# A blocked transpose on one core: three load slots and two store regions, where there were two and three

## The chip, the cores and the metric

The kernel runs on one core of a Trainium2 chip. The core has five engines that run their own instruction streams: PE (TensorE, here used only to transpose), ACT (ScalarE) and DVE (VectorE), which here only copy, POOL (GpSimd), which here only makes an identity matrix, and SP (SyncE), which here issues every data transfer. Sixteen DMA engines move the data between DRAM and the core's on-chip memory of 128 partitions. PE writes into a second on-chip memory, PSUM. Semaphores order the engines among each other. The metric is the device time of one execution in microseconds; lower is better.

## The reference

```python
def setup_inputs():
    return {"x": np.random.randn(8192, 8192).astype(np.float32)}

def reference(x):
    return np.transpose(x)
```

Every one of the 268.44 MB of x is read once and written once, to the transposed place.

## The kernel before

**Tiles.** x is cut into 128 tiles (T) of 128 rows by 4096 columns: 64 chunks of rows (CH) for the first half of the columns, then 64 for the second. A load (L190) brings one tile of 2 MB, 16 KB per partition. The 4096 columns of a tile are 16 ranges (NR) of 256 columns. PE transposes each range in two steps of 128 by 128 (L346), even columns and odd columns, so that a partition holds two neighbouring rows of the result. Ranges 0 to 7 go to the PSUM tensor `ps0`, which ACT empties, ranges 8 to 15 to `ps1`, which DVE empties (`copies`, L252). A range of one tile, transposed, is a *piece*: 1 KB per partition (`PIECE` = 256 floats).

**Regions.** One piece would be written as runs of 512 bytes. So 16 pieces of one range, from 16 tiles that follow each other, are collected in a *region* and stored together (`store`, L288), in runs of 8 KB. Region w belongs to range w % 16 and takes the pieces of tiles w-15 to w: with each tile exactly one region is closed. The piece of tile w is its *closing piece*; it is copied from PSUM straight into the region (`direct`, L224). The other fifteen waited in the tensor `slots`; DVE brings them into the region with one or two copies (`gather`, L227). After the last tile fifteen regions are left with fewer than 16 pieces each; these are the last stores (`flush`, L97). Where a region reaches over the change from the first half of the columns to the second, it is stored in two transfers.

**Memory.** The tensor `arena` has 86 pieces (86 KB) per partition. In it lie load slots of 16 pieces each and the space for regions. At the start there are four load slots, at 0, 16, 54 and 70; the last two are given up early (`over`, L79), and from tile 11 on loads alternate between two slots, at 0 and 16. The pieces from 32 on, 54 of them (`FIN`), are for regions: three full regions follow each other at 32, 48 and 64. A plan made while the program is built (L102 to L147) fixes where each load and each region lies (`home`) and which earlier users of that place must be done (`before`): for a load, that PE has finished the tile that lay there; for a region, that the store of what lay there has landed.

**Order.** SP issues loads and stores from one list (`order`, L102) on one queue: the store of region t-1, the load of tile t+2 (t+4 and t+3 at the start, `lead`, L70), the store of region t, and so on. SP waits at each for its semaphores, so what stands behind waits too. On DVE, `work` (L372) gives for each tile: the gather of its region (which waits until the place is free, then until both engines' copies of the tile before are done), and then the copies of `ps1`. ACT copies `ps0`; it waits for the gather first, since the region's place must be free before the closing piece goes there. Both take their copies in the order of the ranges, as PE finishes 4 ranges (`steps`, L173). The store of a region waits for all copies of the half that has its closing piece (`s_cp`, L292).

**PE's program.** The transposes of tiles 0 to 11 (E = 12) are written out. Tiles 12 to 125 run in a loop whose body is two tiles (L361 to L365), because the load slots alternate by two; it has 57 turns. Tiles 126 and 127 are written out again. For each tile PE waits for the load (L343) and, twice, for an emptied half of PSUM (L341).

Of the kernel before, what the change touches and what calls it, by code (L numbers as in the profile page):

```python
# [40 lines left out]
def kernel(  # L41
# [5 lines left out]
    nc = tc.nc  # L47
    P = 128
# [4 lines left out]
    B = 2  # L53
    NR = 16
# [2 lines left out]
    CH = N // P  # L57
    T = (M // J) * CH
    PIECE = B * P
    FIN = 54  # L60
    QR = NR // 4
    E = 12
    assert CH % W == 0

    FOUR, THREE = 5, 10
    END = 2 * NR + FIN

    def lead(t):  # L70
        return 4 if t < FOUR else 3 if t < THREE else 2


    line = {}
    for t in range(T):
        for u in range(t + lead(t) + 1):
            line.setdefault(u, u if t == 0 and u < 4 else line.get(u - lead(t)))
    ends = sorted((max(t for t in range(T) if t in line and line[t] == v), v) for v in range(4))
    over = [t + 1 for t, _ in ends]  # L79
    slot_of = {ends[0][1]: 54, ends[1][1]: 70, ends[2][1]: 0, ends[3][1]: NR}  # L80

    def spot(t):
        return slot_of[line[t]]
# [35 lines left out]
    for k in order:  # L119
        if k[0] == "L":  # L120
            wanted.append((due[k] - 2 * NR, k, NR, due[k] + 2 * NR))
        elif k[1] < T:
            w = k[1]
# [6 lines left out]
    for _, k, size, until in sorted(wanted):  # L130
        if k[0] == "L":
            o = spot(k[1])
        else:
            w = k[1]
            lo = 2 * NR if w < T - 1 else 0
            hi = 54 if w < over[0] else 70 if w < over[1] else END
            late = lambda o: max([f for _, a, z, f in users if a < o + size and o < z], default=0)
            o = min(range(lo, hi - size + 1), key=lambda o: (late(o), o))
        home[k] = o
        before[k] = sorted({u for u, a, z, _ in users if a < o + size and o < z}, key=lambda u: due[u])  # L140
        users = [
            (u, c, d, f)
            for u, a, z, f in users
            for c, d in ((a, min(z, o)), (max(a, o + size), z))
            if c < d
        ]
        users.append((k, o, o + size, until))  # L147

    with tc.tile_critical():  # L149
        ident = nc.alloc_sbuf_tensor("ident", [P, P], dt).ap()  # L150
        nc.alloc_sbuf_tensor("pad", [P, 64], dt)
        slots = nc.alloc_sbuf_tensor("slots", [P, (NR * (NR - 1) // 2) * PIECE], dt).ap()
        arena = nc.alloc_sbuf_tensor("arena", [P, END * PIECE], dt).ap()
        pss = [nc.alloc_psum_tensor(f"ps{k}", [P, J // 2], dt).ap() for k in range(2)]

        s_id = nc.alloc_semaphore("s_id")
        s_ld = {o: nc.alloc_semaphore(f"s_ld{o}") for o in (0, 16, 54, 70)}
        s_st = [nc.alloc_semaphore(f"s_st{k}") for k in range(2 * W - 1)]
        s_pe = nc.alloc_semaphore("s_pe")
        s_free = [nc.alloc_semaphore("s_fra"), nc.alloc_semaphore("s_frv")]  # L160
        s_cp = [nc.alloc_semaphore("s_cpa"), nc.alloc_semaphore("s_cpv")]
        s_g = nc.alloc_semaphore("s_g")
        s_x = nc.alloc_semaphore("s_x")

        stored = [0] * (2 * W - 1)
        done = {}
        ready = {}
        begun = {}
        gathered = [0]

        def steps(t):  # L173
            return (2, 4, 8, 12, 16) if t == T - 1 else (4, 8, 12, 16)

        def range_at(t, g):
            return (t + g) % NR if t == T - 1 else g
# [16 lines left out]
        def place(w, t):  # L194
            base = home["S", w] * PIECE
            for a, z in parts(w):
                if a <= t < z:
                    return base + (t - a) * P, (z - a) * P
                base += (z - a) * PIECE

        def slot(r, t):
            m = t % W
            d = (r - m) % W
            if d < W // 2:
                return ((d - 1) * W + m) * PIECE
            if d > W // 2:
                return ((W - d - 1) * W + r) * PIECE
            return ((d - 1) * W + min(r, m)) * PIECE

        def ap(tensor, off, dims):  # L210
            return bass.AP(tensor.tensor, tensor.offset + off, [list(tensor.ap[0])] + dims)

        def runs_of(cells_, key):
            runs = []
            for v in cells_:
                if runs:
                    r = runs[-1]
                    if key(r[-1], v) is not None and (len(r) == 1 or key(r[-1], v) == key(r[0], r[1])):
                        r.append(v)
                        continue  # L220
                runs.append([v])
            return runs

        def direct(w, t):  # L224
            return t == w or (t == T - 1 and w == T)
# [26 lines left out]
        def copies(t):  # L252
            for e, eng in enumerate((nc.scalar, nc.vector)):
                need = max(ready[w] for w in (t, T) if w in ready and direct(w, t))
                if need:
                    eng.wait_ge(s_g, need)
                lo = e * NR // 2
                for n, hi in enumerate(steps(t)):
                    if hi <= e * NR // 2 or hi > (e + 1) * NR // 2:
                        continue  # L260
                    eng.wait_ge(s_pe, 4 * t + n + 1)  # L261
                    cells_ = []
                    for g in range(lo, hi):
                        r = range_at(t, g)
                        w = t + (r - t) % NR
                        cells_.append((g, w, None if direct(w, t) else slot(r, t)))
                    for v in runs_of(cells_, lambda a, b: None if None in a + b else b[2] - a[2]):
                        g, w, o = v[0]
                        u = g - e * NR // 2
                        i = pss[e][:, u * PIECE:(u + len(v)) * PIECE]  # L270
                        if o is None:
                            off, dist = place(w, t)
                            dst = ap(arena, off, [[dist, B], [1, P]])
                            i = i.rearrange("p (b i) -> p b i", b=B)
                        else:
                            gap = v[1][2] - o if len(v) > 1 else PIECE
                            dst = ap(slots, o, [[gap, len(v)], [1, PIECE]])
                            i = i.rearrange("p (l i) -> p l i", l=len(v))
                        cp = eng.copy(out=dst, in_=i) if e == 0 else eng.tensor_copy(out=dst, in_=i)  # L279
                        if t == T - 1 and o is None and w == t:  # L280
                            cp.then_inc(s_x, 1)
                    lo = hi
                cp.then_inc(s_cp[e], 1)
                if t < T - 1:
                    eng.wait_ge(s_cp[e], t + 1)
                    eng.sem_inc(s_free[e], 1)  # L286

        def store(w):  # L288
            if w == T - 1:
                nc.sync.wait_ge(s_x, 1)  # L290
            elif w < T:
                nc.sync.wait_ge(s_cp[w % NR // (NR // 2)], w + 1)  # L292
            else:
                if w == T:
                    nc.sync.wait_ge(s_cp[0], T)
                nc.sync.wait_ge(s_g, ready[w])
            pieces = []
            base = home["S", w] * PIECE
            r = w % NR
            for a, z in parts(w):  # L300
                s, c = divmod(a, CH)
                rows = (z - a) * P
                j0 = s * J + r * PIECE
# [12 lines left out]

        first = 0
        while order[first] == ("L", first) and not before[order[first]]:
# [6 lines left out]
            out=ident,  # L325
            in_=ident,
# [25 lines left out]
                    tr.then_inc(s_pe, 1)  # L352

        nc.tensor.wait_ge(s_id, 2)
        for t in range(E):
            transposes(t)
        pe = [nc.tensor.engine]
# [1 line left out]
        nc.regs_mov(turn, 0)  # L359
        nc.br("turns", engines=pe)  # L360
        with nc.body("turns", valid_engines=pe):  # L361
            for t in range(E, E + 2):
                transposes(t)
            nc.regs_alu(turn, turn, 1, op=mybir.AluOpType.add)
            nc.tensor.br_lt(turn, (T - 2 - E) // 2, on_true="turns", on_false="done")  # L365
        nc.switch_bb("done")
        for t in range(T - 2, T):
            transposes(t)

        worked = [0]  # L370
# [53 lines left out]
```

## Time and profile before

| What | Value |
|---|---|
| median of 3 runs | 1270.98 us (1270.83 to 1271.13) |
| the profiled execution | 1270.35 us |
| its span, first to last instruction | 1268.5 us |
| PE / DVE / ACT busy | 58% / 49% / 21% |
| DMA | 537.09 MB, mean 423 GB/s |
| mean granted clock of PE | 0.744 |

The page of the profile gives the busy time of each engine, the span in 40 slices, the DMA queues, and the groups of instructions by source line; L190 is line 190 of the kernel. PEld is PE's loading of weights, which runs beside its matmuls. A name with q behind it (SPq, PEldq) is the engine's sequencer, which waits, branches and issues. "A <- B" in a list of waits reads: A waited, and B ended the wait; the numbers are the total in us, how often, and the longest. q1 is the queue on which SP issues the data transfers; q8 and q14 are queues of the kind "instruction". The rows that windows give have, for each engine, the busy us and in brackets the count of instructions, then PE's granted clock, the busy share of the DMA engines and the GB/s that they moved.

### The profile page before, as it was taken

What the parts mean: (1) busy time and instruction counts of PE and PEld (TensorE: products, weight loads), DVE (VectorE), ACT (ScalarE), POOL (GpSimd) and SP (SyncE); (2) the same over time, 40 slices, a digit from 0 to 9 for tenths busy, and PEclk for the clock granted to TensorE, in tenths of its full rate; (3) what the DMA queues carried; (4) which work ended last, traced back from release to release, by engine and by line L of the source; (5) the groups of instructions that cost most, each with busy time, mean ns of one, the idle gap of its engine ahead of it and who ended that gap; (6) DMA issues with size and microseconds to landing.
All of it is one profiled execution on the core that took longest, in us unless ns stands there. A gap on an engine that the chain in (4) does not pass through costs nothing. (4 is left out here: it accounts for less than half of the span.)

```text
span 1268.5 us, 10842 instructions
## 1 busy us (share of the span) xinstructions
PE 739.7 (58%) x4096; PEld 719.2 (57%) x4096; DVE 615.3 (49%) x715; ACT 268.1 (21%) x402; POOL 0.7 (0%) x6
## 2 busy tenths in 40 slices
PE   6767555655566556565566556565566555665540
PEld 6657555655556556555566555564566555565530
DVE  3553554455445544445444554445444455445561
ACT  3321221222222122211222112221122211221110
POOL 0000000000000000000000000000000000000000
PEclk9986777686877867867767767768767767768765
DMA  9999999999999999999999999999999999999998
GB/s 394 415 426 427 431 429 430 430 430 431 432 430 430 430 431 418 432 426 422 429 423 419 427 428 430 429 420 422 425 419 423 430 423 422 430 423 425 430 421 343
DMA packets 41332, 537.09 MB, mean 423 GB/s; under 512 B 4576, under 2 KB 5216, under 8 KB 8288
## 3 DMA queue, kind: packets, MB, share of 16 engines
q1 hardware_dynamic: 41312, 536.89, 100.0%
q14 instruction: 16, 0.13, 0.0%
q8 instruction: 4, 0.07, 0.0%
HBM read 268.44 MB, written 268.44 MB: 423 GB/s over the span
## 5 line engine op out<-in xcount | busy, mean ns | idle before, releaser
L346 PE MATMUL ps<-ident,arena 128*128 128x128 f32 x4096 | 739.7, 363 | 482.1 <-PEq L343 482.1
L346 PEld LDWEIGHTS ps<-ident,arena 128*128 128x128 f32 x4096 | 719.2, 219 | 502.4 <-issue 502.4
L279 DVE COPY slots<-ps 128x512 f32<-128x512 f32 (+2 forms) x336 | 294.2, 915 | 537.8 <-PE ps L346 537.7
L279 ACT COPY slots<-ps 128x1024 f32<-128x1024 f32 (+2 forms) x335 | 252.7, 773 | 880.6 <-PE ps L346 832.9
L243 DVE COPY arena<-slots 128x2048 f32<-128x2048 f32 (+7 forms) x316 | 304.1, 1012 | 54.2 <-DVE slots L279 29.1
L279 DVE COPY arena<-ps 128x256 f32<-128x256 f32 x63 | 26.2, 416 | 37.8 <-PE ps L346 37.8
L279 ACT COPY arena<-ps 128x256 f32<-128x256 f32 x66 | 24.8, 378 | 70.2 <-PE ps L346 55.0
L279 ACT ACT_TABLE_LOAD x1 | 1.3, 1283 | 1.0 <-SPq L149 1.0
L324 POOL TENSOR_SCALAR_AFFINE_SELECT ident<-ident 128x128 f32<-128x128 f32 x1 | 0.3, 292 | 0.2 <-POOL ident L322 0.2
L322 POOL MEMSET ident<- 128x128 f32 x1 | 0.2, 204 | 0.5 <-SPq L149 0.5
L408 POOL MEMSET const-bfloat16-1.0<- 128x1 bf16 x1 | 0.1, 101 | 0.0
L408 POOL MEMSET const-uint8-127<- 128x1 uint8 x1 | 0.1, 101 | 0.0
L408 POOL MEMSET const-float32-0.0<- 128x1 f32 x1 | 0.1, 98 | 0.2 <-issue 0.2
L408 POOL MEMSET const-float32-1.0<- 128x1 f32 x1 | 0.1, 98 | 0.0
## 6 DMA issues: line engine op xcount, KB each, us to landing
arena<-in_x_dram SPq DMA_DIRECT2D x128, 2048.0 KB, 13.8
out_dram<-arena SPq DMA_DIRECT2D x98, 2048.0 KB, 17.6
out_dram<-arena SPq DMA_DIRECT2D x4, 1920.0 KB, 14.2
out_dram<-arena SPq DMA_DIRECT2D x4, 1792.0 KB, 13.6
out_dram<-arena SPq DMA_DIRECT2D x4, 1664.0 KB, 14.8
out_dram<-arena SPq DMA_DIRECT2D x4, 1536.0 KB, 14.3
out_dram<-arena SPq DMA_DIRECT2D x4, 1408.0 KB, 13.8
out_dram<-arena SPq DMA_DIRECT2D x4, 1280.0 KB, 16.3
```

What stands on the lines that cost most here:

```text
L243: cp = nc.vector.tensor_copy(out=ap(arena, do, [[P, len(v)], [dist, B], [1, P]]), in_=ap(slots, so, [[gap, len(v)], [P, B], [1, P]]),)
L279: cp = eng.copy(out=dst, in_=i) if e == 0 else eng.tensor_copy(out=dst, in_=i)
L322: nc.gpsimd.memset(ident, 0.0).then_inc(s_id, 1)
L324: nc.gpsimd.affine_select(out=ident, in_=ident, compare_op=mybir.AluOpType.not_equal, fill=1.0, base=0, pattern=[[-1, P]], channel_multipl ...
L346: tr = nc.tensor.transpose(pss[h][:, (u * B + b) * P:(u * B + b + 1) * P], arena[:, q + b:q + PIECE - B + b + 1:B], ident,)
L408: nc = _bacc.Bacc("TRN2", target_bir_lowering=False, num_devices=1)
```

## The change

The `arena` keeps its 86 pieces, but is divided otherwise: three load slots, at 0, 16 and 32, for the whole run, a fourth at 70 for the start alone, and 38 pieces for regions, in which two full regions alternate, at 48 and 70. The load of tile t+2 now takes the place of tile t-1 instead of tile t. The region of tile w takes the place of region w-2 instead of w-3. The regions of the last two tiles and the last fifteen may lie in load slots; region 126 is put where tile 125 lay.

Copies: each engine first builds the list of its copies of a tile and puts the closing piece ahead of the others; runs of pieces are still not joined across PE's steps. The closing copy raises a semaphore of its own (`s_x`), and a store waits for that instead of `s_cp`. The engines wait for the gather before their copies, as before.

PE's loop has three tiles in its body instead of two, since load slots now rotate by three: tiles 12 to 125 in 38 turns, and tiles 126 and 127 written out.

SP's list of loads and stores is the same, and DVE's sequence of gathers and copies has the same instructions but for the order inside a tile.

```diff
-    FIN = 54
+    FIN = 38
+    NIN = 3
...
-    END = 2 * NR + FIN
+    END = NIN * NR + FIN
...
-    for t in range(T):
-        for u in range(t + lead(t) + 1):
-            line.setdefault(u, u if t == 0 and u < 4 else line.get(u - lead(t)))
-    ends = sorted((max(t for t in range(T) if t in line and line[t] == v), v) for v in range(4))
-    over = [t + 1 for t, _ in ends]
-    slot_of = {ends[0][1]: 54, ends[1][1]: 70, ends[2][1]: 0, ends[3][1]: NR}
+    for u in range(T):
+        line[u] = u if u < 4 else line[u - (4 if u < FOUR + 4 else 3)]
+    ends = sorted((max(u for u in range(T) if line[u] == v), v) for v in range(4))
+    over = ends[0][0] + 1
+    slot_of = {v: k * NR for k, (_, v) in enumerate(ends[1:])}
+    slot_of[ends[0][1]] = END - NR
...
-            lo = 2 * NR if w < T - 1 else 0
-            hi = 54 if w < over[0] else 70 if w < over[1] else END
+            lo = NIN * NR if w < T - 2 else 0
+            hi = END - NR if w < over else END
             late = lambda o: max([f for _, a, z, f in users if a < o + size and o < z], default=0)
-            o = min(range(lo, hi - size + 1), key=lambda o: (late(o), o))
+            at = range(lo, hi - size + 1)
+            if over <= w < T - 2:
+                at = (lo, hi - size)
+            elif w == T - 2:
+                at = [spot(T - 3)]
+            o = min(at, key=lambda o: (late(o), o))
...
-                lo = e * NR // 2
-                for n, hi in enumerate(steps(t)):
-                    if hi <= e * NR // 2 or hi > (e + 1) * NR // 2:
-                        continue
+                first, last = e * NR // 2, (e + 1) * NR // 2
+                cells_ = []
+                for g in range(first, last):
+                    r = range_at(t, g)
+                    w = t + (r - t) % NR
+                    n = next(n for n, hi in enumerate(steps(t)) if g < hi)
+                    cells_.append((g, w, None if direct(w, t) else slot(r, t), n))
+                runs = runs_of(
+                    cells_, lambda a, b: None if None in a + b or a[3] != b[3] else b[2] - a[2]
+                )
+                runs.sort(key=lambda v: v[0][1] != t)
+                for v in runs:
+                    g, w, o, n = v[0]
                     eng.wait_ge(s_pe, 4 * t + n + 1)
...
-                        if t == T - 1 and o is None and w == t:
-                            cp.then_inc(s_x, 1)
-                    lo = hi
+                    if w == t:
+                        cp.then_inc(s_x[e], 1)
+                        shut[e] += 1
+                        closed[t] = (s_x[e], shut[e])
...
-            if w == T - 1:
-                nc.sync.wait_ge(s_x, 1)
-            elif w < T:
-                nc.sync.wait_ge(s_cp[w % NR // (NR // 2)], w + 1)
+            if w < T:
+                nc.sync.wait_ge(*closed[w])
...
+        LAST = T - 1 - (T - 1 - E) % NIN
...
-            for t in range(E, E + 2):
+            for t in range(E, E + NIN):
                 transposes(t)
             nc.regs_alu(turn, turn, 1, op=mybir.AluOpType.add)
-            nc.tensor.br_lt(turn, (T - 2 - E) // 2, on_true="turns", on_false="done")
+            nc.tensor.br_lt(turn, (LAST - E) // NIN, on_true="turns", on_false="done")
...
-        for t in range(T - 2, T):
+        for t in range(LAST, T):
             transposes(t)
```

More of the change, by code (lines that the diff above doesn't have):

```diff
@@ L156 @@
         s_id = nc.alloc_semaphore("s_id")
-        s_ld = {o: nc.alloc_semaphore(f"s_ld{o}") for o in (0, 16, 54, 70)}
+        s_ld = {o: nc.alloc_semaphore(f"s_ld{o}") for o in sorted(slot_of.values())}
         s_st = [nc.alloc_semaphore(f"s_st{k}") for k in range(2 * W - 1)]
@@ L162 @@
         s_g = nc.alloc_semaphore("s_g")
-        s_x = nc.alloc_semaphore("s_x")
+        s_x = [nc.alloc_semaphore("s_xa"), nc.alloc_semaphore("s_xv")]
         stored = [0] * (2 * W - 1)
@@ L169 @@
         gathered = [0]
+        closed = {}
+        shut = [0, 0]
         def steps(t):
@@ L256, in copies @@
                     eng.wait_ge(s_g, need)
-                lo = e * NR // 2
-                for n, hi in enumerate(steps(t)):
-                    if hi <= e * NR // 2 or hi > (e + 1) * NR // 2:
-                        continue
-                    eng.wait_ge(s_pe, 4 * t + n + 1)
[L262 to L279, printed above, removed]
-                        if t == T - 1 and o is None and w == t:
-                            cp.then_inc(s_x, 1)
-                    lo = hi
@@ new lines, in copies @@
+                runs.sort(key=lambda v: v[0][1] != t)
+                for v in runs:
+                    g, w, o, n = v[0]
+                    eng.wait_ge(s_pe, 4 * t + n + 1)
+                    u = g - first
+                    i = pss[e][:, u * PIECE:(u + len(v)) * PIECE]
+                    if o is None:
+                        off, dist = place(w, t)
+                        dst = ap(arena, off, [[dist, B], [1, P]])
+                        i = i.rearrange("p (b i) -> p b i", b=B)
+                    else:
+                        gap = v[1][2] - o if len(v) > 1 else PIECE
+                        dst = ap(slots, o, [[gap, len(v)], [1, PIECE]])
+                        i = i.rearrange("p (l i) -> p l i", l=len(v))
+                    cp = eng.copy(out=dst, in_=i) if e == 0 else eng.tensor_copy(out=dst, in_=i)
+                    if w == t:
+                        cp.then_inc(s_x[e], 1)
+                        shut[e] += 1
+                        closed[t] = (s_x[e], shut[e])
```

## The prediction

> **What bounds the kernel now.** I read the page first, then the waits of SyncE's queue, then windows of 10 us, then the DMA view cut to windows.
>
> ```profile
> span 1268.5 us, 10842 instructions
> PE 739.7 (58%) x4096; PEld 719.2 (57%) x4096; DVE 615.3 (49%) x715; ACT 268.1 (21%) x402; POOL 0.7 (0%) x6
> GB/s 394 415 426 427 431 429 430 430 430 431 432 430 430 430 431 418 432 426 422 429 423 419 427 428 430 429 420 422 425 419 423 430 423 422 430 423 425 430 421 343
> q1 hardware_dynamic: 41312, 536.89, 100.0%
> q14 instruction: 16, 0.13, 0.0%
> q8 instruction: 4, 0.07, 0.0%
> HBM read 268.44 MB, written 268.44 MB: 423 GB/s over the span
> arena<-in_x_dram SPq DMA_DIRECT2D x128, 2048.0 KB, 13.8
> out_dram<-arena SPq DMA_DIRECT2D x98, 2048.0 KB, 17.6
> ```
>
> No compute engine is over 58% busy; the one data queue, q1, fills 100.0% of sixteen DMA engines' time. The kernel reads and writes each byte once, so 536.89 MB at 423 GB/s is the span. A transfer of 2,048 KB takes 2.097 MB / 423 GB/s = 5.0 us of all engines, and a load lands 13.8 us after its issue, a store 17.6 us: two to three other transfers stand ahead of each. A tile (one load, one store) is thus 9.9 us, and whatever SyncE, PE, DVE or ACT do inside that time is hidden as long as the queue keeps something ahead. The best slice, 432 GB/s, would give 1243 us: nothing done to waits can win more than 25 us.
>
> ```profile
> SPq L190 <- PE ps L346: 975.4, 124, 11.4
> SPq L28 <- DVE slots L279: 83.2, 56, 9.4
> 480.35 2.42 DVE L279 COPY slots<-ps 128x1024 f32<-128x1024 f32 x3 [4.92 <-PE ps L346]
> 481.30 0.33 SPq L190 DMA_DIRECT2D arena<-in_x_dram  x1
> 481.68 0.66 SPq L28 DMA_DIRECT2D out_dram<-arena  x1
> 483.01 2.43 DVE L243 COPY arena<-slots 128x2048 f32<-128x2048 f32 x3 [0.24 <-DVE slots L279]
> 484.76 6.55 PE L346 MATMUL ps<-ident,arena 128*128 128x128 f32 x32 [3.50 <-PEq L343]
> 860.00:870.00 10.00, 5.36 (x34) 5.19 (x33) 5.15 (x6) 2.08 (x3) 0.00 (x0) 0.84 0.99 398
> 970.00:980.00 10.00, 5.45 (x34) 5.29 (x33) 4.78 (x5) 2.15 (x4) 0.00 (x0) 0.84 1.00 428
> ```
>
> SyncE spends its time in the wait of a load for PE to finish the tile two before (975.4 us in 124 waits, 7.9 us each). The reader is to see that this longest wait costs little: in the two windows the DMA engines are 0.99 and 1.00 busy, though one moves 398 GB/s and the other 428. What is lost is lost inside packets, not between them.
>
> **The change, part by part.**
>
> *Third load slot.* A load now waits for PE's tile three before, which is over; the 7.9 us go. Late next is the store ahead of it in SyncE's order, which still needs PE's tile, the gather and one copy. So load and store leave as a pair about when the store left before. On the DMA engines I take 0: both transfers already queue for 9 to 13 us beyond their own 5.0 us. The ends: no loss, and a gain of at most the low windows, 1100 us x (1 - 427/432) = 12.7 us between 100 and 1200 us:
>
> ```profile
> DMA packets 34452, 469.34 MB, mean 427 GB/s; under 512 B 3832, under 2 KB 4088, under 8 KB 5624
> q1 hardware_dynamic: 34439, 469.24, 100.7%
> q14 instruction: 13, 0.11, 0.0%
> ```
>
> *Two store regions instead of three.* The gather of store w now needs store w-2 landed instead of w-3. The chain is store issue, landing, gather 2.43 us, closing copy 0.4 us, issue 0.5 us; it must close in two tiles, 19.7 us. With the median landing it would be 17.6 + 3.3 = 20.9 us, too long; but a landing is mostly queue. With fewer transfers ahead, near the end (the first two rows are the window 1204 to 1214 us):
>
> ```profile
> q1 hardware_dynamic: 290, 4.23, 99.2%
> out_dram<-arena SPq DMA_DIRECT2D x1, 2048.0 KB, 11.7
> L279 DVE COPY arena<-ps 128x256 f32<-128x256 f32 x63 | 26.2, 416 | 37.8 <-PE ps L346 37.8
> L279 ACT COPY arena<-ps 128x256 f32<-128x256 f32 x66 | 24.8, 378 | 70.2 <-PE ps L346 55.0 <-DVE arena L243 15.3
> ```
>
> a store of the same size lands in 11.7 us, and 11.7 + 3.3 = 15.0 us leaves 4.7 us. The queue pays by standing shorter, the engines do not. I take 0; the ends are 0 and (20.9 - 19.7)/2 x 110 tiles = 66 us if landings did not shrink.
>
> *Copies after the gather, closing piece first.* The copies are as many as before (401 on ACT, 715 with the gathers on DVE). The store waits for one copy (0.4 us) instead of its half's copies (2.42 us in the row of 480.35 us): up to 2 us earlier, hidden by the same queue. Behind the waiting gather on DVE stand the copies of ps1, and ACT's wait for the gather too, so PSUM is handed back later: gather 2.43 and copies 2.4 us after the landing of store t-2, which follows load t by one transfer, 5.0 us: 9.8 us after load t. PE's next load comes after 9.9 us. That cover is thin, but PE itself has 482.1/127 = 3.8 us of idle time per tile behind it (row below), so 0, and at most 1 us of a store's issue, again inside the queue.
>
> *Last regions in load slots.* Region 126 waits for PE's tile 125 instead of store 123, region 127 for store 124 as before; the last fifteen stores wait for the same kind of thing. The drain ran with engines full, so 0, and no more than the shortfall of the two windows against 432, 0.5 us, either way:
>
> ```profile
> 1240.00:1250.00 10.00, 0.00 (x0) 0.00 (x0) 3.90 (x5) 0.00 (x0) 0.00 (x0) 0.50 1.01 418
> 1250.00:1260.00 10.00, 0.00 (x0) 0.00 (x0) 0.00 (x0) 0.00 (x0) 0.00 (x0) 0.50 1.01 421
> ```
>
> *PE's loop.* This part has a price. The loop over tiles 12 on has three tiles in its body instead of two, because the load slots rotate by three. Queue q8 moved 4 packets in the whole run, and the windows show when:
>
> ```profile
> L346 PE MATMUL ps<-ident,arena 128*128 128x128 f32 x4096 | 739.7, 363 | 482.1 <-PEq L343 482.1
> L341 PEldq EVENT_SEMAPHORE  x256: 51/51/671, 1.0 to 1215.3; - x128
> L343 PEldq EVENT_SEMAPHORE  x128: 51/51/51, 8.3 to 1215.1; - x128
> L365 PEldq COMPARE_BRANCH  x57: 76/208/227, 98.7 to 1198.7; - x57
> 69.20:73.00 3.80, 3.72 (x23) 3.75 (x24) 1.16 (x2) 0.00 (x0) 0.00 (x0) 0.70 1.01 431
> 1205.30:1209.00 3.70, 3.64 (x17) 3.67 (x18) 0.66 (x1) 1.01 (x1) 0.00 (x0) 0.50 1.00 430
> q1 hardware_dynamic: 5, 0.08, 100.2%
> q8 instruction: 1, 0.02, 28.2%
> ```
>
> The last two rows are the window 1208.9 to 1209.1 us. The third q8 packet came in the 11th tile after 23 transposes (73.0 us), the fourth in tile 126 after 17 (1209.0 us), and between them, through all 57 turns of the loop, none: the rows of 100 to 1200 us above have no q8. In the program tile 126 is the 15th tile written out (12, then the body's 2), so the packets lie 14 x 32 + 17 - (10 x 32 + 23) = 122 transposes apart. [...] The point that brought the fourth lies behind the old body, in transposes 0 to 17 of the 15th tile. In the changed program the 15th tile is the third of the body. So each of the (126 - 12)/3 = 38 turns passes that point and then jumps back across it; the old body held no such point.
>
> One such packet took 28.2% x 16 x 0.2 us = 0.90 us of one DMA engine. How many a turn needs no row shows. The least is none (the code is still there), the next one (each passing so far brought one). [...] 38 x 3 x 0.90 us = 103 us of engine time, over 16 engines 6.4 us. That is when the packets fall on all engines alike; the other end is that a block always comes through the same engine, 38 x 0.90 = 34 us on each of three. As every transfer ends with its slowest engine, that engine's loss would be the kernel's. I take the even one, because the window 1204 to 1214 us, which holds the fourth packet, still moved 4.23 MB in 10 us on q1, 423 GB/s as the mean of the run; 34 us stays for the range. [...]
>
> [...]
>
> **Sum.** 0 + 0 + 0 + 0 + 6.4 us on the profiled execution's 1270.35 us (span 1268.5 and 1.85 around it): 1276.8. The median of the runs, 1270.98, is 0.63 above it: 1277.4 us.
>
> **The rivals.**
>
> 1. *The code stays in PE* (no fetch in the loop). [...] All other terms are 0: 1271 us, within 0.2% (2.5 us, about what a measurement of this kernel can tell from no change). It is also the case that the change does not do what it says: loads leave earlier and nothing comes of it.
> 2. *Each block comes through one engine.* Then 0.62 (by bytes, 16,384 B at 423/16 GB/s) to 0.90 us x 38 on single engines, 24 to 34 us: 1294 to 1305. Nothing in the views names the engine of a packet.
> 3. *Faster: the low windows fill.* If the 398 to 420 GB/s windows come from engines that wait for the next load's issue, 7.9 us earlier loads end that, 12.7 us at most: 1258 if the loop costs nothing. It decides only where the wait of the load outlasts what stands in the queue. Against it is the busy share of 0.99 in the lowest of them.
> 4. *The two-region chain becomes the bound.* From 19.7 us per two stores on it sets the pace: up to 66 us, 1337. Against it is the landing of 11.7 us.
>
> **How the numbers follow.** Even fetches, 1273.5 to 1284: 0.42. One engine per block, 1284 to 1305: 0.24. No fetch, 1268.4 to 1273.5: 0.22. Low windows fill: 0.07. Chain, or more than 34 us of fetches: 0.05. Slower 0.42 + 0.24 + 0.05 = 0.71, same 0.22, faster 0.07. The range 1268 to 1305 leaves out the last two cases, 0.12; the likeliest alone has 1273 to 1284.
>
> **What would show it.** q8 with some 4 + 114 packets, 1.9 MB, spread over the whole span (4 to 5 packets: rival 1; about 42: one fetch a turn). [...] SyncE's wait of the load's line for PE falls from 975 us to nearly nothing, and its wait at the store's line takes most of it. The gather waits for out_dram in nearly every tile, and ACT's copies for the gather. The prediction is wrong if q8 stays at 4, or if GB/s over 100 to 1200 us rises above 430.

## The result, and the profile after

The changed kernel takes 1326.22 us in the median of 4 runs (1319.75 to 1355.38), against 1270.90 for the kernel before (4 runs). The longest of the four is a slow run and stays out of the comparison: the other three have a median of 1323.69, a ratio of 1.042, 95% interval 1.0375 to 1.0464. The change costs some 53 us. Forecast were 1277.4 us with a range of 1268 to 1305: the time is outside the range, and the cause is another than the one that was forecast, so that the right sign is luck. The profiled execution took 1323.69 us.

The page of the changed kernel, the rows that answer to those of the kernel before:

```profile
span 1321.9 us, 10802 instructions
PE 742.1 (56%) x4096; PEld 721.4 (55%) x4096; DVE 614.6 (46%) x715; ACT 257.3 (19%) x402; POOL 0.7 (0%) x6
GB/s 390 419 420 429 428 428 428 431 431 431 430 432 431 430 431 431 431 431 428 428 429 429 431 426 419 414 404 397 387 366 372 364 363 374 362 365 369 365 329 346
q1 hardware_dynamic: 41312, 536.89, 98.0%
q14 instruction: 16, 0.13, 0.0%
q8 instruction: 4, 0.07, 0.0%
HBM read 268.44 MB, written 268.44 MB: 406 GB/s over the span
L251 DVE COPY arena<-slots 128x2048 f32<-128x2048 f32 (+7 forms) x316 | 304.1, 1011 | 644.6 <-DMA out_dram<-arena 637.3
arena<-in_x_dram SPq DMA_DIRECT2D x128, 2048.0 KB, 21.1
out_dram<-arena SPq DMA_DIRECT2D x98, 2048.0 KB, 16.9
```

Three things are to be seen. q8, whose packets the prediction took for PE's code, still has 4 of them: the packets that made up the whole of the predicted loss did not come. The GB/s row (slices of 33 us) is flatter than before from 100 to 760 us, 428 to 432 without the dips to 418 and 419 that the kernel before has there, and then falls to about 365 within 200 us and stays there. So the loss is not spread over the run; it belongs to the last third. And the gather (L251 now) waits 637.3 us for stores to land. In the kernel before, this wait was 19.1 us in all:

```profile
DVE arena L243 <- DMA out_dram<-arena: 19.1, 5, 5.8
```

The waits of the changed kernel, first of the whole core and then of SyncE's queue:

```profile
DVE arena L251 <- DMA out_dram<-arena: 637.3, 118, 11.3
ACT slots L289 <- DVE arena L251: 507.8, 62, 13.5
ACT arena L289 <- DVE arena L251: 481.1, 61, 9.6
```

```profile
SPq L28 <- DVE arena L289: 541.9, 62, 10.5
SPq L28 <- ACT arena L289: 507.6, 58, 10.4
SPq L198 <- PE ps L355: 50.4, 10, 12.0
```

The load's wait for PE (L198) has gone from 975.4 us to 50.4. In its place SyncE waits at the store (L28) for the closing copy, 1049.5 us in 120 waits, that copy waits for the gather, and the gather waits for the landing of store t-2. One chain now sets when SyncE issues anything: landing, gather, closing copy, store, load, landing. Here it is in the timeline, once while the rate is 431 GB/s and once while it is 366:

```profile
490.37 2.43 DVE L251 COPY arena<-slots 128x2048 f32<-128x2048 f32 x3 [4.99 <-DMA out_dram<-arena]
492.83 0.37 ACT L289 COPY arena<-ps 128x256 f32<-128x256 f32 x1 [7.88 <-DVE arena L251]
493.23 0.54 SPq L28 DMA_DIRECT2D out_dram<-arena  x1
493.81 0.59 SPq L198 DMA_DIRECT2D arena<-in_x_dram  x1
503.12 0.54 SPq L28 DMA_DIRECT2D out_dram<-arena  x1
...
1106.53 0.55 SPq L28 DMA_DIRECT2D out_dram<-arena  x1
1107.12 0.59 SPq L198 DMA_DIRECT2D arena<-in_x_dram  x1
1115.06 2.29 DVE L251 COPY arena<-slots 128x2048 f32<-128x2048 f32 x3 [6.51 <-DMA out_dram<-arena]
1117.39 0.37 ACT L289 COPY arena<-ps 128x256 f32<-128x256 f32 x1 [9.27 <-DVE arena L251]
1117.79 0.55 SPq L28 DMA_DIRECT2D out_dram<-arena  x1
```

From the landing to the end of the store's issue it is 2.43 + 0.03 + 0.37 + 0.03 + 0.54 = 3.4 us early and 2.29 + 0.04 + 0.37 + 0.03 + 0.55 = 3.3 us late. What has changed is the time from one landing to the next: stores follow each other after 9.9 us at first (493.23, 503.12) and after 11.3 us late (1106.53, 1117.79). The windows of 80 us around the two places:

```profile
480.00:560.00 80.00, 46.76 (x257) 45.47 (x256) 39.08 (x45) 15.98 (x25) 0.00 (x0) 0.75 1.01 431
1095.00:1175.00 80.00, 40.27 (x224) 39.14 (x224) 33.51 (x41) 13.98 (x25) 0.00 (x0) 0.74 0.94 366
```

The granted clock of PE is the same (0.75, 0.74) and so is a transpose, 46.76/257 = 0.182 us against 40.27/224 = 0.180. In the second window the DMA engines have gaps: 0.94 busy.

What grows in between is not in any view of the page. The trace has, for each transfer, the sixteen times at which its sixteen shares landed, one for each DMA engine. These are the first landing (us) and, behind it, the sixteen distances from it:

```
changed kernel
 load  460.06  0  0.05 0.14 0.15 0.20 0.46 0.59 0.60 0.83 0.97 2.68 2.77 3.56 3.58 3.94  5.54
 store 474.66  0  0.06 0.15 0.16 0.20 0.46 0.58 0.60 0.86 0.97 2.67 2.77 3.58 3.60 3.99  5.82
 store 1056.07 0  0.02 0.03 0.07 0.10 0.19 0.29 0.30 0.31 0.37 0.40 0.48 0.58 0.64 0.65 13.04
kernel before
 store 1036.85 0  0.14 0.16 0.19 0.29 0.38 0.39 0.52 0.62 0.68 0.69 2.36 2.70 2.92 3.76  5.82
```

One engine lags behind the others. The next table follows that lag, the distance from first to last landing of a store, by the store's number; in brackets about how far the last landing is behind a run at the common pace of 4.86 us for a 2 MB transfer (8 packets of 16 KB per engine, which start 607 ns apart; each is recorded as 611 ns long). The bracketed figures hold to about 1 us over the whole run, their differences from row to row to about 0.2. The rows below the second belong to the experiments. Stores 64 to 78 go out as two transfers each, which widens the distance for a while, so none of them is in the table.

```
store          24         47         56         79         87         104        120        124
before      3.8 (5.8)  5.7 (7.7)  5.8 (8.9)  5.7 (11.6) 5.8 (12.7) 5.9 (15.7) 5.4 (17.7) 5.5 (18.2)
after       3.3 (6.3)  5.4 (8.4)  6.7 (9.7)  9.3 (12.4) 10.3 (14.3) 13.0 (37.4) 13.0 (64.8) 12.9 (71.6)
e2_memory   2.9 (9.6)  5.1 (11.5) 6.4 (12.8) 7.6 (16.4) 9.8 (20.5) 10.4 (44.4) 10.3 (66.3) 10.3 (71.8)
e4_waits    4.0 (7.9)  5.1 (8.9)  4.1 (11.8) 6.8 (14.6) 7.9 (15.7) 5.8 (20.2) 9.4 (23.6) 9.8 (24.3)
e5_brake    3.6 (10.9) 4.4 (11.7) 5.6 (12.9) 5.7 (17.6) 5.6 (19.0) 5.4 (21.4) 5.6 (24.5) 5.8 (25.1)
e6_two_reg. 2.9 (5.1)  5.7 (8.5)  5.8 (9.9)  6.1 (12.8) 5.8 (13.9) 5.6 (17.0) 5.5 (19.1) 5.8 (19.7)
e9_one_wait 3.8 (6.7)  5.1 (7.9)  6.3 (9.1)  3.8 (14.8) 4.4 (15.9) 7.2 (18.7) 9.5 (20.9) 9.6 (21.4)
e10_late_b. 2.9 (7.2)  5.3 (9.6)  6.6 (10.8) 5.1 (14.0) 5.5 (15.7) 5.8 (18.2) 5.8 (20.4) 6.1 (21.5)
```

In the kernel before the lag stays near 6 us (5.1 to 6.6 from store 47 on, two-transfer stores aside). In the changed one it rises by 0.12 us a tile from store 47 to store 79, stands at 9.3 to 9.7 up to store 85, and then the kernel falls behind: (71.6 - 12.4) - (18.2 - 11.6) = 52.6 us against the kernel before in 45 tiles, which is nearly the whole loss of 53.

**The theory that the experiments test.** One DMA engine needs longer for stores, 4.99 us instead of 4.86, and so falls 0.13 us behind with each tile. In the kernel before, a load waits until PE has finished the tile two before, and PE needs that tile from the slow engine too. This wait is a brake: it holds the next load back for the fifteen others too until the slow one has caught up, and the lag stays near 6 us. By this theory it costs nothing, as the slow engine hardly stands for it: its last landing falls back by (18.2 - 5.8)/100 = 0.12 us a tile, about the 0.13 that it loses by itself. The third load slot takes the brake away. Then the next wait that counts all sixteen shares is the gather's, for the landing of store t-2. When its last share lands, a load, a store and a load stand behind it, 3 x 4.86 = 14.6 us of work on each engine, of which the fast engines have done as much as the lag. The new store needs 3.4 us until it is issued and some 0.65 us more until its first packet on an idle engine (issue of 1106.53 done at 1107.08, packets from 1107.73 on). So the fast engines run dry at a lag of 14.6 - 3.4 - 0.65, about 10.5 us. (The expectations below were written with about 9 us, which is nearer to where the packets begin to lengthen.)

The trace comes close to this. From store 82 on, at a lag of 9.6 us, many packets of the fast engines get longer than 611 ns, up to some 1400, and the rate begins to fall. At store 93, with a lag of 11.8 us at the store two before, several engines stand idle for the first time, and from store 100 on all fifteen stand at once for 0.3 to 0.6 us in each tile (970.01 to 970.52 us is the first; from the first of them to stand to the last it is 969.7 to 970.6).

### The profile page after: what moved, and what is told of

It is laid out like the page before. It is cut to its first block, busy times and chain, and to the rows that moved or that the text cites. A ratio compares the mean times of both kernels' runs of the same rounds, so it can differ in the third digit from the quotient of the medians.

```text
span 1321.9 us, 10802 instructions
## 1 busy us (share of the span) xinstructions
PE 742.1 (56%) x4096; PEld 721.4 (55%) x4096; DVE 614.6 (46%) x715; ACT 257.3 (19%) x402; POOL 0.7 (0%) x6
## 5 line engine op out<-in xcount | busy, mean ns | idle before, releaser
L251 DVE COPY arena<-slots 128x2048 f32<-128x2048 f32 (+7 forms) x316 | 304.1, 1011 | 644.6 <-DMA out_dram<-arena 637.3
L289 ACT COPY slots<-ps 128x1024 f32<-128x1024 f32 (+2 forms) x335 | 238.3, 781 | 513.3 <-DVE arena L251 507.8
L289 DVE COPY slots<-ps 128x512 f32<-128x512 f32 (+2 forms) x336 | 289.0, 911 | 30.8 <-PE ps L355 28.9
## 6 DMA issues: line engine op xcount, KB each, us to landing
out_dram<-arena SPq DMA_DIRECT2D x98, 2048.0 KB, 16.9
out_dram<-arena SPq DMA_DIRECT2D x4, 1920.0 KB, 11.8
out_dram<-arena SPq DMA_DIRECT2D x4, 1792.0 KB, 11.8
```

The costliest lines, as they stand in the source:

```text
L251: cp = nc.vector.tensor_copy(out=ap(arena, do, [[P, len(v)], [dist, B], [1, P]]), in_=ap(slots, so, [[gap, len(v)], [P, B], [1, P]]),)
```

## The experiments

The kernel before was run beside them and took 1270.45, 1270.92 and 1270.73 us (medians of 16, 17 and 13 runs).

**The copies alone.** The kernel before, with the new order of the copies, the closing copy's own semaphore and the store's wait for it. Memory and PE's loop stay.

```diff
-                lo = e * NR // 2
-                for n, hi in enumerate(steps(t)):
...
+                runs.sort(key=lambda v: v[0][1] != t)
...
+                    if w == t:
+                        cp.then_inc(s_x[e], 1)
...
-                nc.sync.wait_ge(s_cp[w % NR // (NR // 2)], w + 1)
+                nc.sync.wait_ge(*closed[w])
```

> The kernel before with the new order of copies and the new wait of the store alone (two load slots, three regions, loop of two tiles). Theory A (one DMA engine falls behind at every store; with two regions the next store waits for that engine, and once it is about 9 us behind, the other fifteen run dry): 1269 to 1273 us, since the gather never waits for a landing. Theory B (the copies that now stand behind the gather make PE late): 1300 us or more, as in the changed kernel.

Measured: 1270.34 us, 0.9999 (0.9988 to 1.001). The copies cost nothing and bring nothing.

**The memory alone.** The changed kernel with the copies and the store's wait of the kernel before (the same diff, backwards); three load slots, two regions and the loop of three tiles stay.

> The changed kernel with the old order of copies and the old wait of the store: three load slots, two regions. Theory A: slow as the changed kernel or slower, 1320 to 1370 us, because the store leaves 2 us later after the gather and so the others run dry at a lag of 7 us instead of 9, some 15 tiles earlier. Theory B: about 1271 us.

Measured: 1320.59 us (2 runs), 1.040 (1.0334 to 1.0467). The GB/s row of its page:

```profile
GB/s 391 418 396 412 423 432 430 430 431 430 431 431 429 433 430 432 431 429 429 425 422 417 419 430 424 400 386 376 384 377 381 372 373 387 375 374 380 378 366 334
```

and the gather's wait among its waits:

```profile
DVE arena L251 <- DMA out_dram<-arena: 633.3, 117, 11.7
```

The memory plan with its loop carries the whole loss, with the same picture: flat, then a fall from about 800 us on. The longer way from landing to store (some 2 us more) was expected to start the fall some 15 tiles earlier, at a lag lower by 2 us. The lag came out so: engines first stand idle in number at store 88, with 9.5 us at the store two before, against 11.8 in the changed kernel. The tiles were a miss, as that is only 5 tiles earlier, and the row then stays at 372 to 387 where the changed kernel has about 365. The order of the copies shifts the fall, it doesn't make it.

**PE's loop alone.** The kernel before, with 14 tiles written out ahead of the loop instead of 12. The loop of two tiles then covers the place in PE's program that brought the fourth packet on q8, and passes it in each of its turns.

```diff
-    E = 12
+    E = 14
```

> The kernel before with 14 tiles of PE's program written out instead of 12, so that the loop's two tiles lie across the point at which PE fetched its fourth block. Theory A: 1269 to 1273 us and 4 packets on q8. Theory C (the step of the prediction: every turn fetches code again): 1275 us or more and over 100 packets on q8.

Measured: 1270.83 us, 1.0003 (0.9991 to 1.0014).

```profile
q8 instruction: 4, 0.07, 0.0%
```

Passing that place in each turn brings one packet, the first time, and none after. In the changed kernel the trace has the fourth packet at 108.5 us, while the transposes of the first turn still run; the other 37 turns brought none. (There PE's sequencer, ahead of its transposes, had jumped back at 107.6 us; in this run the packet comes at 108.3 and the first jump at 115.0, so that here the place lies inside the loop for certain.) The term of the predicted sum is refuted, at no cost measured.

**Two added waits.** The changed kernel, in which stores 48 and 88 also wait until the store before them has landed. Everything is as in the changed kernel, with two waits more.

```diff
             if w < T:
                 nc.sync.wait_ge(*closed[w])
+                if w in (48, 88):
+                    nc.sync.wait_ge(s_st[lane(w - 1)], done[w - 1])
```

> The changed kernel with two more waits in SyncE's queue: stores 48 and 88 also wait until the store before them has landed on all sixteen engines. That holds the fifteen fast engines back for some us, once each, and takes work from none. Theory A: the lag never reaches 9 us, 1270 to 1280 us, and no window under 415 GB/s but for the two. Theory D (two regions make the chain of landing, gather, copy and issue too long for two tiles, lag or no lag): 1320 us or more, as without the waits.

Measured: 1276.41 us (3 runs), 1.0053 (1.003 to 1.0076). Two more waits make the changed kernel some 47 us faster. The GB/s row, the wait of SyncE's queue at the added line (L303), and the late window:

```profile
GB/s 393 416 404 425 429 430 430 433 430 432 429 431 431 431 394 428 428 431 430 428 428 428 423 430 432 430 368 427 430 429 429 431 431 429 430 429 426 428 381 333
```

```profile
SPq L303 <- DMA out_dram<-arena: 31.4, 2, 15.7
```

```profile
1095.00:1175.00 80.00, 44.69 (x259) 43.39 (x258) 38.50 (x44) 16.05 (x26) 0.00 (x0) 0.80 1.01 429
```

The reader is to see two slices with a dip (394 and 368 GB/s, the two waits, 15.7 us at most on SyncE) and no fall at the end: in the window in which the changed kernel moves 366 GB/s, this one moves 429. During the waits the fast engines stand and the slow one catches up; the lag is 5.1 us at store 47 and 2.7 at 48, 7.9 at 87 and 2.7 at 88. No other part of the kernel was touched, so the fall is a matter of what has gathered by then.

**The brake put back.** The changed kernel, in which a load from tile 13 on also waits for PE to finish the tile two before, though a third slot is free.

```diff
+            if t > 12:
+                free(nc.sync, ("L", t - 2))
```

> The changed kernel with the old wait of a load put back: from tile 13 on a load also waits until PE is done with the tile two before, as with two slots. Theory A: that wait was the brake which kept the fifteen engines within 6 us of the slow one, short of the 9 us at which the two-region chain runs them dry: 1269 to 1274 us. Theory E (the new places in the arena or the new chain alone are slow): 1300 us or more.

Measured: 1278.73 us (4 runs), 1.006 (1.003 to 1.009). The GB/s row, SyncE's wait at the brake (L189), and the gather's wait:

```profile
GB/s 395 414 382 410 427 430 429 430 431 432 431 430 432 431 430 431 431 425 431 401 419 416 429 421 420 425 429 424 432 419 420 429 428 414 421 431 424 426 419 348
```

```profile
SPq L189 <- PE ps L357: 851.4, 115, 8.8
```

```profile
DVE arena L253 <- DMA out_dram<-arena: 586.3, 117, 11.4
```

With the load's wait back (851.4 us) the lag stays near 6 us (at most 6.4, two-transfer stores aside), the dips of the kernel before return, and the fall is gone, although the gather still waits 586.3 us for landings. That is the theory's main claim. The time is some 5 us over the expected 1269 to 1274; slices 2 and 3 (counted from 0: 382 and 410 GB/s, the kernel before has 426 and 427) hold most of it, ((426 - 382) + (427 - 410))/430 x 32 = 4.5 us. Whether the brake makes that dip isn't settled: the run of the memory alone (396, 412) and the one with two waits (404, 425) have a smaller one there without a brake.

**Two regions alone.** The kernel before with its two load slots, in which full regions from number 16 on lie at 32 and 64 alone, so that a gather waits for store t-2.

```diff
-            o = min(range(lo, hi - size + 1), key=lambda o: (late(o), o))
+            at = (32, 64) if 16 <= w < T - 2 else range(lo, hi - size + 1)
+            o = min(at, key=lambda o: (late(o), o))
```

> The kernel before with two full regions, at 32 and 64, from region 16 on, and everything else as it was (two load slots). Theory A: the loads' wait still brakes, 1269 to 1274 us; the gather waits for landings, but the DMA engines do not run dry. Theory E (two regions alone make it slow): 1300 us or more.

Measured: 1271.89 us, 1.0008 (0.9996 to 1.0019). The GB/s row, the gather's wait (L244), and the load's wait in SyncE's queue (L191):

```profile
GB/s 392 416 427 432 426 432 430 432 430 431 430 431 424 430 429 409 431 430 422 429 424 423 426 428 414 429 426 421 430 417 421 430 430 418 430 416 431 430 420 338
```

```profile
DVE arena L244 <- DMA out_dram<-arena: 568.4, 115, 7.3
```

```profile
SPq L191 <- PE ps L347: 696.7, 124, 11.9
```

The gather waits 568.4 us for landings in 115 of the tiles, nearly as much as in the changed kernel, and nothing is lost: the load's wait for PE (696.7 us) is still there, and the lag stays near 6 us. Two regions are harmless while the loads are braked. By the theory the third slot harms because nothing else holds the fast engines back before the landing's chain does. The third slot with three regions, which would show it alone, was not run: it needs 3 x 16 + 3 x 16 = 96 pieces, and the arena has 86.

**One engine relieved.** If an engine has more work than it can do, taking work from it should help. In the kernel before and in the changed one, stores 24, 50 and 90 are issued as two transfers, of 8 and of 120 partitions, so that one engine could be left out of part of the work.

```diff
+                if w in (24, 50, 90):
+                    st = wide_dma(nc, nc.sync, "qSPDynamicHW", dst[120:], src[120:])
+                    st.then_inc(s_st[lane(w)], 16)
+                    stored[lane(w)] += 16
+                    dst, src = dst[:120], src[:120]
```

> The kernel before, with stores 24, 50 and 90 issued as two transfers of 8 and of 120 partitions. 120 partitions should go to fifteen engines and leave one out, which then does 5 us less each time. Theory A with the slow engine being that one: its 18 us of delay shrink by up to 15, and the next slowest engine sets the end: 1257 to 1265 us. If another engine is left out: 1270 to 1274 us, and nothing follows for the theory.

> The changed kernel with the same three stores split. Theory A with the slow engine being the one left out: its lag never reaches 9 us, so the stall does not begin: 1257 to 1266 us. If another engine is left out: 1315 to 1360 us, as the changed kernel.

Measured: 1276.01 us for the kernel before (8 runs), 1.004 (1.0024 to 1.0057), and 1289.36 for the changed one (2 runs), 1.0138 (0.9997 to 1.0278). Neither expectation was met. In the kernel before the splits cost 5 us, in the slices where they lie (down to 413, 400 and 394 GB/s); what a split itself costs can't be told from a relief of the slow engine by the time alone. The landings tell more. A split store has 23 landings of data, eight and fifteen, so one engine was indeed left out of the 120 partitions. In the changed kernel the distance from first to last landing rose by it, from 3.4 us at store 23 to 8.2 at store 26, since the engine left out now lands 2.0 us ahead of the next. These 2.0 us are the same at store 39, where a slow engine would have lost 13 x 0.13 = 1.7 of them, while the last engine goes on falling behind. So the engine left out is not the slow one, and the runs name no engine beyond that. What a relief would bring stays untested.

The changed kernel with splits is faster than without (1296.84 and 1281.87 us; two runs are too few to say by how much), and not because the lag is low: it is 9.4 us at store 47, where the changed kernel has 5.4, and then stands at 9.4 to 9.7 from store 79 to 105, except near the split at 90. In that stretch the rate stays at 422 to 429 GB/s outside the dips of the splits (414, 415, 403); it falls for good only after 1036 us, as the lag passes 10. Here the other engines are spread: at store 100 the fifteen land within 4.5 us, in the changed kernel within 0.6. So a distance of 9.5 us is not yet a loss, and it seems to matter how many engines have gathered at the front (a reading of these two traces, not tested).

**One wait.** As the run with two waits, with a single one at store 66, to tell a lag that gathers from a place in the work that is slow.

```diff
+                if w == 66:
+                    nc.sync.wait_ge(s_st[lane(w - 1)], done[w - 1])
```

> The changed kernel with one added wait instead of the two of the run with waits at 48 and 88: store 66 also waits until store 65 has landed. Theory (the lag of one DMA engine behind the others grows by some 0.13 to 0.15 us a tile, and from about 9 us on the other fifteen run dry): the lag falls from some 7 us to some 3 us at tile 66, reaches 9 us about 43 tiles later, near tile 109, so that the last 15 to 20 tiles still lose 1.2 us each: 1271 + 3 for the wait + 18 to 24, that is 1296 us (1286 to 1306), and the slices of GB/s fall below 415 only after about 1090 us. Rival (the loss belongs to a place in the work, from tile 79 on, whatever the lag): 1310 to 1326 us, with the slices low from 800 us on. Rival (one clearing is enough): 1272 to 1276.

Measured: 1276.20 us (4 runs), 1.0049 (1.0032 to 1.0066). The GB/s row of its page:

```profile
GB/s 392 416 424 424 428 430 428 432 431 431 430 431 432 430 431 431 431 431 430 379 391 419 425 428 430 430 428 431 431 430 431 431 429 431 433 429 430 431 380 334
```

The rival of a slow place is out: after the dip of the wait (379, 391) the rate comes back, and from slice 24 (763 us) to the drain there are 428 GB/s and more, through all tiles in which the changed kernel is slow. The theory's number was a miss by 20 us, and the rival that one clearing is enough (1272 to 1276) was nearest. The lags show why: they were expected to grow from tile 66 on, but after a rise to 6.6 us and back among the two-transfer stores they stood at 3.8 to 4.4 us from store 79 to 87, and then grew by (9.5 - 4.4)/33 = 0.155 us a tile. It came to 9.6 us just as the loads ended, and so cost nothing. That agrees with a fall that begins between 9.5 and 10 us, as in the runs with two waits (9.8 at the end, no fall) and without (the first falling slices at 9.5 to 10.3).

**The brake from tile 65 on.** As the brake above, begun later.

```diff
-            if t > 12:
+            if t > 64:
                 free(nc.sync, ("L", t - 2))
```

> The changed kernel whose loads wait, from tile 65 on only, also for PE to finish the tile two before, as in the kernel before (in the run with this brake on all loads from tile 13 on: 1278.7 us, of which slices 2 and 3 lost some 5). Theory: the lag of the slow DMA engine stays under 9 us for the rest, as the brake begins at some 7 us, and the two low slices at 64 to 128 us are gone: 1270 to 1275 us. Rival (the brake comes too late, the lag has to be held down from the start): over 1285. Rival (the 8 us of the earlier brake are the two-region chain itself): 1277 to 1281, with the lost time spread over the slices.

Measured: 1273.41 us (10 runs), 1.0016 (1.0007 to 1.0026). The GB/s row and SyncE's wait at the brake:

```profile
GB/s 393 416 407 425 426 432 428 430 429 430 431 431 430 431 432 429 431 432 413 414 421 422 426 426 426 430 418 428 429 406 432 429 424 424 429 424 431 420 407 350
```

```profile
SPq L189 <- PE ps L357: 462.9, 63, 8.3
```

The lag of 7.3 us at store 62 is brought down, and held at 4.7 to 6.3 from store 79 on; there is no fall, and 5 us of the earlier brake's 8 are gone. So the third slot, the two regions, the copies, the last regions and the loop of three together cost 2.7 us when the fast engines can't run ahead from tile 65 on, and without that some 53. No version was faster than the kernel before.

## Why the prediction was wrong, step by step

- **PE's loop, +6.4 us: the failing term of the sum.** It measured 0. The place in the program was read rightly to within some transposes (the fourth packet came after 17 transposes of the 15th tile in the kernel before and after 19 in the changed one; the third came after 343 and 352 in all). But the three packets a turn in 38 x 3 x 0.90 us had no row, and no run shows them: the runs showed one packet for this place, at its first passing, and none after, with 4 on q8 in both the changed kernel and the run of the loop alone, where 38 and 56 turns passed it. Rival 1, no fetch in the loop, was right on this point. That q8's packets are PE's code is the author's reading of the places at which they come; where the code lies between two passings no run shows.
- **Two regions, 0 us: the failing step behind the size.** The place was named (rival 4: the chain landing, gather, closing copy, issue "becomes the bound", 66 us, 1337), but it had a share of 0.05. That its price is near the 53 us measured is luck: it spreads 0.6 us a tile over 110 tiles, where the runs show nothing up to store 80 and then, once the fall is complete, some 1.5 us a tile. The dismissal read "a landing is mostly queue" and took 11.7 us, from a store near the end. Up to store 80 the queue did pay "by standing shorter": a store's last share landed 16.9 us after its issue, the store two after it was issued 2.9 us later, and 19.8 us are two tiles. What it left out is that a landing counts when the slowest of sixteen engines is done. From store 100 on the last share lands 19.8 to 20.3 us after the issue, and with 2.8 to 2.9 us behind it the chain takes 22.6 to 23.1 us for two tiles. The page's median of 16.9 us hides this, and with it the up to 13 us between first and last landing.
- **Third slot, 0 us.** Its working was right (the load's wait went to 50.4 us, the store's wait took it, both leave as a pair), and its consequence was not seen: the wait that was removed held the engines together. "What is lost is lost inside packets, not between them" describes the trace (in the window of 398 GB/s, 24 of the 243 packets of 16 KB took 719 to 1876 ns instead of 611), but what was drawn from it, that the wait has no part in it, was the misreading that hid this. The dips are gone in the changed kernel from 100 to 760 us, so they hung on the load's wait. Rival 3 was thus right that the low windows fill, and wrong that time is won: at store 79 the last landing stands 12.4 us behind, 11.6 in the kernel before, since the slow engine sets the end either way.
- **Copies, 0 us:** right, measured 1270.34 with them alone. The closing copy's gain did not matter there. Behind a gather that waits for landings, the copies were not tried apart from the rest; the run with the late brake bounds them, as the next part.
- **Last regions, 0 us:** not tried alone; in the run with the late brake all parts together cost 2.7 us, which bounds it.
- **What would show it:** the move of SyncE's wait from the load to the store, the gather's wait for landings in nearly every tile (118) and ACT's wait for the gather came as forecast. q8 with 118 packets didn't, and it had been named as the sign by which the prediction is wrong.

What stays open: once the fifteen have run dry, the slow engine alone should still set the old pace of 9.9 us, and it doesn't. Its own packets get longer near the issues (single ones of 2147 and 2278 ns at 1095 and 1118 us instead of 611), and a load takes it 6.3 to 6.6 us instead of 4.86, while its stores still take 5.0: these 1.5 us are the loss of a tile. The loss grows as the engines gather at the front: the fifteen land within 4.4 us of each other at store 79, within 2.8 at 96 and within 0.6 at 100. The runs show when this begins and that holding the engines together ends it, not why the sixteenth's loads take longer once the fifteen have stood. Nor is it settled which engine is the slow one.

## What to carry to other kernels

A wait that looks idle and long (975.4 us here) may be what keeps the sixteen DMA engines in step; before it is removed, look for the next wait that counts all sixteen shares of a transfer, and compare first and last landings over the run (here 5.4 us apart at store 47 and 13.0 at store 104), not the median from issue to landing (16.9). A loss that shows only in the last third of a uniform loop can be a quantity that gathers: here a single added wait in the middle, one cheap run, told it from a slow place (1276.20 us, where 1310 to 1326 were expected of the slow place). A chain that is bounded by a landing is to be priced with the slowest engine's landing late in the run (19.8 to 20.3 us here), since a landing that was measured with short queues (11.7) didn't show how far the engines had drifted apart.

## What the runs showed of the hardware

- One of the sixteen DMA engines is slower, and in stores only: 16 KB packets of 615 to 644 ns where the others take 611, and 0.13 us more for 2 MB (4.99 instead of 4.86), in both kernels, while its loads go at the common pace, 4.86 us, as long as the others do not run dry (6.3 to 6.6 us after that). The records don't name the engine; that it is one and the same is read from the last landings, which follow each other by these times.
- By this reading the engine bounds the kernel before: its last landing is 5.8 us behind the common pace at store 24 and 18.2 at store 124, (18.2 - 5.8)/100 = 0.12 us a tile. By this estimate some 12 of the 1270 us are this engine's.
- The busy share of the DMA engines hides lost time: it is 0.99 at 398 GB/s in the kernel before (860 to 870 us), where packets took up to 1876 ns. What such a packet waits for isn't shown: most of the long ones begin at 862 to 864 us, 4 us and more after the last issue (857.81), with that store still to be moved, and before the next (865.01). Only at 366 GB/s did the share fall, to 0.94, with the fifteen engines idle at once for 0.3 to 0.6 us in each tile.
- In the two runs in which the body of PE's loop covers the place that brings a 16 KB packet on q8, that packet came once: 4 packets on q8 in all, with 56 turns of two tiles and with 38 turns of three.
